# Two more pairs of w2 k tiles in Strassen's form, and two plain pairs whose lo parts arrive by accumulating transfers

## The chip, the cores and the metric

The kernel runs on one core of a Trainium2 chip. The metric is the device time of one execution in microseconds (us), taken from the first to the last instruction; the kernel before was timed in three runs. One more execution was profiled, and every duration below is from that one. PE is the matrix engine, DVE the Vector engine, ACT the Scalar engine, POOL is GpSimd, and SP is the engine that only issues transfers.

## What is computed

Two layers of a decoder trunk over 256 tokens of width 1024, in float32. Each layer is a feed-forward block, a mixer (gated spatial unit beside differential attention) and a second feed-forward block, each followed by a layer norm. The change touches the four feed-forward blocks alone:

```python
def _swiglu(x, w1, w3, w2):
    return (jax.nn.silu(x @ w1) * (x @ w3)) @ w2
...
for l in range(DEPTH):
    h = _swiglu(x, ffn_w1[l, 0], ffn_w3[l, 0], ffn_w2[l, 0])
    x = _layernorm(ALPHA * x + 0.5 * h, ln_g[l, 0], ln_b[l, 0])
    h = _mixer(x, ...)
    x = _layernorm(ALPHA * x + h, ln_g[l, 1], ln_b[l, 1])
    h = _swiglu(x, ffn_w1[l, 1], ffn_w3[l, 1], ffn_w2[l, 1])
    x = _layernorm(ALPHA * x + 0.5 * h, ln_g[l, 2], ln_b[l, 2])
```

The inner width of a feed-forward block is 2816, which is 22 tiles of 128.

## The kernel before

**Three matmuls for one.** A float32 operand is split into a hi part, rounded to a shorter format by ACT (a copy), and a lo part, the remainder, which DVE gets by a subtraction. `three` (L208) then issues hi·hi, lo·hi and hi·lo into one PSUM bank. Weights come from memory as float32 tiles of 128x2048 (1 MB) into one of four `raw` buffers, by a transfer on SP's queue, and are cut there: ACT writes the hi half tile (128x1024), DVE the lo half tile. There are eight hi and eight lo buffers of 128x1024. A `raw` buffer is free for the next transfer when its last cut is done; a hi or lo buffer is free when PE has read it for the last time.

**A feed-forward block** has an up stage and a down stage. The up stage (`gemm_b2`, then `gemm_a2` for nine pairs of inner tiles) makes the 22 inner tiles, and splits each into hi and lo. The down stage multiplies them with w2. A *plain pair* is two inner tiles with 24 matmuls of 128x512: two tiles, two token halves t, two column halves c, three matmuls each (`rows_p`, six matmuls at a time). A *Strassen pair* does the same product with seven blocks in place of eight, so 21 matmuls. Its inner operands are mixed by `mixed` (L559), and its weights by `stream_s` (L280): one raw tile is cut into a (512 columns, L304), b (1024), c (1024) and d (1024), and DVE adds quarters of the raw tile in place between the cuts (L306, L308, L309), so that cut d can be made only after L309, first its hi by ACT and then its lo by DVE. The seven blocks are issued in the order 3, 7, 4, 1, 2, 5, 6 (L631); block 3 and 2 read cut b, 7 and 5 read c, 4 and 6 read d, and 1 reads a. Block 4, the seventh to ninth matmul of the pair, is thus the first to need d, its lo in the eighth matmul. The seven blocks of all Strassen pairs add up in seven banks `S`.

**The down stage's order.** There are `NS = 4` Strassen pairs and seven plain ones. The order on PE is Strassen, plain, Strassen, plain, Strassen, plain, Strassen (L629 to L635). The other four plain pairs are *held*: all of their weights are cut and kept in the hi and lo buffers (eight of each), and PE then goes through (t, c) = (0,0), (0,1), (1,0), (1,1), each with all held pairs (L648 to L655), so that the sums of the first token half are complete when half of the held work is still to come. Beside that, DVE adds the `S` banks to the residual (`more`, L465 and L463; `u`, `v`, L640 and L641) and the four finished banks (`part`, L472), and the layer norm is done for one token half at a time (`finish`, L481).

**From the norm to the next stage.** `finish` starts a task, `turned` (L515), that counts in beats: each `rows_p` or `rows_b` of six matmuls is half a beat, and five of them after (0,1) PE transposes the first half of the normed tokens (L532). ACT scales them into `xf` (L538) and makes the hi part of x, DVE the lo part (L177). The next stage's first matmuls read these. So that the next stage's weights can be cut while the eight buffers still hold the held pairs, its first three half tiles are written to activation slots (`lent = [(0, 1), (0,), (), ()]`, L323; 31 slots of 128x512 in all).

**Order.** PE's order is the program's order, written by hand. A scheduler orders ACT, DVE and POOL ahead of time by priorities; on the chip each engine runs its list strictly in that order, and an instruction that waits holds up all that stand behind it.

## Time and profile before

| | |
|---|---|
| Median of three runs (lowest, highest) | 1230.86 us (1230.62, 1231.16) |
| The profiled execution's own time | 1231.23 us |
| Its span, first to last instruction | 1229.5 us |
| PE busy | 1223.3 us (99%) |
| DVE busy | 980.3 us (80%) |
| ACT busy | 781.1 us (64%) |
| POOL busy | 87.0 us (7%) |
| Granted clock of PE | 1.000 |

The profiled execution is 0.37 us above the median, and 1.7 us of its time lie outside its span. A row of a timeline gives the start, the time to the end of the last of the instructions in it, the engine, the source line, what is written and read, the shape, how many, and in brackets how long the engine was idle before and who ended that. Instructions overlap: the next one starts a little before the end of the one before, so the step from start to start is the rate, and the duration is longer.

### The profile page before, as it was taken

The page shows a single profiled execution, that of the slowest core. Times are in us where ns is not written, and L with a number is a line of the kernel's source. Part 1 is how long each engine was busy: PE and PEld are TensorE (multiplying, and loading weights), DVE is VectorE, ACT ScalarE, POOL GpSimd, SP SyncE. Part 2 cuts the span into 40 slices and gives each one's busy share as a digit, 9 for nine tenths or more (in the row PEclk, how much of TensorE's full clock was granted, in tenths as well). Part 3 has the DMA queues.
Part 4 walks back from the last instruction along what each step waited for, and adds up shares of the span by engine and source line. Part 5 has one row for each costly group of instructions (what it writes and reads, how often), then busy time and mean ns, then how long its engine had stood idle before and what let it go on. Part 6 is the DMA issues. An engine that isn't in the chain of part 4 may idle for free.

```text
span 1229.5 us, 17890 instructions
## 1 busy us (share of the span) xinstructions
PE 1223.3 (99%) x6589; PEld 1050.6 (85%) x6589; DVE 980.3 (80%) x1692; ACT 781.1 (64%) x1424; POOL 87.0 (7%) x184
## 2 busy tenths in 40 slices
PE   9999999999999999999999999999999999999998
PEld 8888888888888888888888888888888888888886
DVE  6877998886587987779978779978866879787886
ACT  6775666679665666656566665566886555766651
POOL 0100000244100000000000000002430000000000
PEclk9999999999999999999999999999999999999999
DMA  9864665654754745546645546656556446455450
GB/s 344 291 205 138 231 217 194 224 167 166 251 178 154 231 159 207 191 138 241 247 178 196 180 142 247 246 188 206 168 174 229 168 171 240 171 206 178 160 211 34
DMA packets 40104, 241.87 MB, mean 197 GB/s; under 512 B 5281, under 2 KB 6353, under 8 KB 13393
## 3 DMA queue, kind: packets, MB, share of 16 engines
q1 hardware_dynamic: 36048, 227.82, 53.2%
q0 software_dynamic: 3536, 12.13, 3.1%
q8 instruction: 51, 0.84, 0.3%
q10 hardware_dynamic: 432, 0.79, 0.2%
q14 instruction: 37, 0.30, 0.1%
HBM read 235.47 MB, written 1.05 MB: 192 GB/s over the span
## 4 chain that ended last, share of the span: by engine, by line
PE 99%; DMA 0%; DVE 0%; ACT 0%; DVEq 0%; issue 0%; ACTq 0%
PE bank L223 38%; PE bank L211 23%; PE bank L230 20%; PE sbank L211 12%; PE bank L371 2%; PE sbank L707 1%; PE sbank L532 1%; PE sbank L756 1%; PE sbank L837 1%; DMA xraw<-in_xT 0%; PE sbank L754 0%; PE sbank L778 0%; PE sbank L585 0%; PE sbank L741 0%; PE sbank L746 0%; PE sbank L504 0%
## 5 line engine op out<-in xcount | busy, mean ns | idle before, releaser
L171 DVE TENSOR_TENSOR wlo<-raw,whi 128x1024 fp32r<-128x1024 f32 (+1 forms) x410 | 450.0, 1116 | 109.1 <-PE bank L230 62.9
L169 ACT ACTIVATE whi<-raw 128x1024 fp32r<-128x1024 f32 (+1 forms) x410 | 388.8, 970 | 186.9 <-PE bank L223 114.8
L223 PE MATMUL bank<-x,whi 128*128 128x512 f32 x1792 | 426.5, 392 | 0.0
L223 PEld LDWEIGHTS bank<-x,whi 128*128 128x128 f32 x1792 | 330.7, 188 | 69.1 <-issue 2.7
L230 PE MATMUL bank<-x,wlo 128*128 128x256 f32 x1792 | 230.0, 284 | 0.0
L230 PEld LDWEIGHTS bank<-x,wlo 128*128 128x128 f32 x1792 | 224.2, 191 | 4.8
L231 ACT ACTIVATE r<-bank 128x256 f32<-128x256 f32 x256 | 96.0, 381 | 67.8 <-PE bank L230 67.4
L211 PE MATMUL bank<-whi,x 128*128 128x512 f32 x328 | 106.6, 394 | 0.0
L293 ACT ACTIVATE shi<-raw 128x1024 fp32r<-128x1024 f32 (+1 forms) x64 | 60.4, 950 | 61.0 <-DVE raw L309 39.1
L295 DVE TENSOR_TENSOR slo<-raw,shi 128x1024 fp32r<-128x1024 f32 (+1 forms) x64 | 69.3, 1088 | 24.8 <-PE bank L230 15.3
L211 PEld LDWEIGHTS bank<-whi,x 128*128 128x128 f32 x328 | 61.6, 188 | 12.7
L211 PE MATMUL sbank<-whi,hhi 128*128 128x512 f32 x168 | 65.7, 391 | 0.0
L211 PE MATMUL sbank<-whi,hlo 128*128 128x512 f32 x168 | 65.4, 389 | 0.0
L211 PE MATMUL sbank<-wlo,hhi 128*128 128x512 f32 x168 | 65.4, 389 | 0.0
L211 PE MATMUL bank<-wlo,x 128*128 128x512 f32 x164 | 64.0, 390 | 0.0
L538 ACT ACTIVATE xf<-sbank,ln_b,ln_g 128x128 f32<-128x128 f32 x80 | 30.1, 456 | 40.8 <-PE sbank L532 40.8
L233 DVE TENSOR_TENSOR silu<-bank,r 128x256 f32<-128x256 f32 x144 | 54.5, 418 | 0.4
L431 POOL DMA_DIRECT2D bc<-in_lng x6 | 3.2, 530 | 728.4 <-DVE bc L430 728.4
L683 POOL TENSOR_TENSOR swap<-swap,sin_t 128x512 f32<-128x512 f32 x16 | 25.0, 1563 | 233.4 <-DMA swap<-z 225.2
L211 PE MATMUL bank<-lhi,x 128*128 128x512 f32 x120 | 39.2, 395 | 0.0
L211 PEld LDWEIGHTS sbank<-whi,hlo 128*128 128x128 f32 x168 | 31.5, 188 | 6.7
L211 PEld LDWEIGHTS sbank<-wlo,hhi 128*128 128x128 f32 x168 | 31.6, 188 | 6.5
(236 smaller groups left out, 1682.3 us busy)
## 6 DMA issues: line engine op xcount, KB each, us to landing
raw<-in_w13a SPq DMA_DIRECT2D x72, 1024.0 KB, 4.9
raw<-in_w2p SPq DMA_DIRECT2D x28, 1024.0 KB, 5.1
raw<-in_wa SPq DMA_DIRECT2D x24, 1024.0 KB, 5.2
raw<-in_w2s SPq DMA_DIRECT2D x16, 1024.0 KB, 4.9
raw<-in_wb SPq DMA_DIRECT2D x16, 1024.0 KB, 5.0
raw<-in_wqk SPq DMA_DIRECT2D x16, 1024.0 KB, 5.2
raw<-in_wbr SPq DMA_DIRECT2D x16, 1024.0 KB, 4.9
raw<-in_w13b SPq DMA_DIRECT2D x12, 1024.0 KB, 5.1
```

The costliest lines, as they stand in the source:

```text
L169: A.activation(h, r, AF.Copy)
L171: V.tensor_tensor(out=w, in0=r, in1=h.bitcast(F32), op=ALU.subtract)
L211: PE.matmul(ps, xx, w, start=start and n == 0, stop=stop and n == 2)
L223: PE.matmul(b[-1], hi[:, k * P : (k + 1) * P], xc(k), start=k == 0, stop=False)
L230: PE.matmul(b[n][:, :T], lo[:, k * P : (k + 1) * P], xc(k)[:, :T], start=False, stop=k == KT - 1)
L231: emptied[0] = A.activation(r[:, s], b[n][:, T:], AF.Copy, scale=scale).ins
L233: a = V.tensor_tensor(out=z[:, s], in0=b[n][:, :T], in1=r[:, s], op=ALU.add)
L293: A.activation(h, r, AF.Copy)
L295: V.tensor_tensor(out=w, in0=r, in1=h.bitcast(F32), op=ALU.subtract)
L371: PE.matmul(ps[t][m], x[:, j, o + t * P : o + (t + 1) * P], y, start=k0 + j == 0 and o == 0 and y is hi, stop=k0 + j == KT - 1 and y is lo)
L538: A.activation(xf[:, s], b[:, s], AF.Identity, scale=self.gT[:, f], bias=self.bT[:, f])
L683: turned_by[0] = G.tensor_tensor(out=s3, in0=s3, in1=s, op=ALU.mult).ins
```

## The change

`NS` becomes 6. The inner tiles 12 to 15 go over from plain to Strassen pairs, so five plain pairs are left, and the order on PE is Strassen, Strassen, plain, Strassen, Strassen, plain, Strassen, Strassen, and then three held pairs. The last Strassen pair's operands lie in the `val` buffers as before, those of the other five in 20 slots.

The first two of the held pairs no longer use the hi and lo buffers. Their weights go to sixteen activation slots, which the finished Strassen pairs have left, in pieces of 128x512. ACT writes each hi piece, and for each lo piece the negated raw value (`scale=-1.0`) in the destination's shorter format; a transfer issued by POOL then reads the same weights from memory a second time and adds them to it in place (`accum_op=ALU.add`), which leaves the remainder. There are eight such transfers of 256 KB in a feed-forward block. DVE has no part in it.

After a feed-forward block `lent` is empty: the next stage's weights all go to the hi and lo buffers. In the up stage a plain pair's two tiles are now collected in `qa` and split at once, 128x512, instead of twice 128x256.

```diff
-NS = 4
+NS = 6
...
-    def stream(src, width=CH, sub=HC, lent=(), after=(None, None)):
+    def stream(src, width=CH, sub=HC, lent=(), after=(None, None), dma=()):
...
                 with behind(latest[0]):
                     A.activation(h, r, AF.Copy)
+                if o // HC in dma:
+                    A.activation(w, r, AF.Copy, scale=-1.0)
+                    G.dma_start(w, src[:, o + p : o + p + sub], accum_op=ALU.add)
+                    continue
                 with behind(after[o // HC] or latest[1]):
                     V.tensor_tensor(out=w, in0=r, in1=h.bitcast(F32), op=ALU.subtract)
...
-            wh, wl = (v[:, j * 512 + c0 : j * 512 + c0 + n] for v in piece)
+            wh, wl = (v[j][:, c0 : c0 + n] if isinstance(v, list) else v[:, j * 512 + c0 : j * 512 + c0 + n] for v in piece)
...
-            lent = [(0, 1), (0,), (), ()]
+            lent = norm.lent
...
+            self.lent = [(0, 1), (0,), (), ()]
...
         for j in range(FB, FT, 2):
+            qa = s512("qa")
             for m, z in gemm_a2([w13a[l, f, j - FB + m] for m in range(2)], both, lambda m: t512("silu")):
                 s = z[:, :T]
                 silu[0] = A.activation(s, s, AF.Silu).ins
-                if (j, j + 1) in SQ:
-                    if m == 0:
-                        qa = s512("qa")
-                    V.tensor_tensor(out=qa[:, m * T : (m + 1) * T], in0=s, in1=z[:, T:], op=ALU.mult)
-                    if m:
-                        mixed((j, j + 1), qa)
-                else:
-                    V.tensor_tensor(out=s, in0=s, in1=z[:, T:], op=ALU.mult)
-                    split(hh(j + m), hl(j + m), s)
+                V.tensor_tensor(out=qa[:, m * T : (m + 1) * T], in0=s, in1=z[:, T:], op=ALU.mult)
+                if m and (j, j + 1) in SQ:
+                    mixed((j, j + 1), qa)
+                elif m:
+                    split(p_hi[j, j + 1], p_lo[j, j + 1], qa)
...
+        ln.lent = [()] * 4
...
-            w = stream(w2p[l, f, PQ.index(q)])
+            slot = hold and len(plain) > 0
+            w = stream(w2p[l, f, PQ.index(q)], sub=512 if slot else HC, lent=(0, 1) if slot else (),
+                       dma=(0, 1) if slot else ())
...
-            if n < NS - 1:
+            if n in (1, 3):
                 plain_pair(False)
```

The diff moves lines, so L306, L308, L309 and L465 of the kernel before are L310, L312, L313 and L470 of the changed one, L295 and L293 are L299 and L297, L171 is L175 and L532 is L537.

Three places in the order of instructions are spoken of below, all in the first feed-forward block; the other three have the same order there. The first is DVE around the last Strassen pair. In the kernel before, the pair's cut d (`slo_1665`) is followed by four cuts of held pairs and then by the first addition of an `S` bank to the residual (`sbank_1425` is the bank of block 7):

```order
L295 TENSOR_TENSOR slo_1663<-raw_1658,shi_1662 128x1024
L308 TENSOR_TENSOR raw_1658<-raw_1658 128x512
L309 TENSOR_TENSOR raw_1658<-raw_1658 128x512
L295 TENSOR_TENSOR slo_1665<-raw_1658,shi_1664 128x1024
L171 TENSOR_TENSOR wlo_1712<-raw_1709,whi_1711 128x1024
L171 TENSOR_TENSOR wlo_1716<-raw_1709,whi_1715 128x1024
L171 TENSOR_TENSOR wlo_1722<-raw_1719,whi_1721 128x1024
L171 TENSOR_TENSOR wlo_1726<-raw_1719,whi_1725 128x1024
L465 SCALAR_TENSOR_TENSOR xtok_144<-xtok_144,sbank_1425 128x512
```

In the changed kernel the same place on DVE reads as follows (`slo_1722` is cut c of the last Strassen pair, `slo_1724` its cut d, `sbank_1436` the bank of block 7):

```order
L299 TENSOR_TENSOR slo_1720<-raw_1717,shi_1719 128x1024
L299 TENSOR_TENSOR slo_1722<-raw_1717,shi_1721 128x1024
L312 TENSOR_TENSOR raw_1717<-raw_1717 128x512
L313 TENSOR_TENSOR raw_1717<-raw_1717 128x512
L470 SCALAR_TENSOR_TENSOR xtok_144<-xtok_144,sbank_1436 128x512
L299 TENSOR_TENSOR slo_1724<-raw_1717,shi_1723 128x1024
L175 TENSOR_TENSOR wlo_1815<-raw_1812,whi_1814 128x1024
```

The addition has moved ahead of cut d of the pair whose block 7 it waits for.

The second place is ACT at the end of the Strassen pairs. In the kernel before, the last pair's cuts b, c and d (`shi_1660`, `shi_1662`, `shi_1664`) stand together, and plain cuts follow:

```order
L293 ACTIVATE shi_1660<-raw_1658 128x1024
L293 ACTIVATE shi_1662<-raw_1658 128x1024
L293 ACTIVATE shi_1664<-raw_1658 128x1024
L169 ACTIVATE whi_1711<-raw_1709 128x1024
L169 ACTIVATE whi_1715<-raw_1709 128x1024
```

In the changed kernel the fifth Strassen pair's cuts c and d (`shi_1681`, `shi_1683`) and then the sixth's b and c (`shi_1719`, `shi_1721`) stand like this on ACT:

```order
L297 ACTIVATE shi_1681<-raw_1675 128x1024
L171 ACTIVATE llo_1772<-raw_1768 128x512
L169 ACTIVATE lhi_1771<-raw_1768 128x512
L171 ACTIVATE llo_1773<-raw_1768 128x512
L169 ACTIVATE lhi_1780<-raw_1768 128x512
L171 ACTIVATE llo_1782<-raw_1768 128x512
L169 ACTIVATE lhi_1781<-raw_1768 128x512
L297 ACTIVATE shi_1683<-raw_1675 128x1024
L297 ACTIVATE shi_1719<-raw_1717 128x1024
L297 ACTIVATE shi_1721<-raw_1717 128x1024
```

Six pieces of the first slot pair (`raw_1768`) now stand between cuts c and d of the fifth pair; six more stand between c and d of the sixth.

The third place is PE between the transposes of the first half of the first token half and the next stage, which is the mixer's. The matmuls that read `x` are the next stage's. In the changed kernel:

```order
L537 MATMUL sbank_1914<-ident,xtok_143 128x128 x4
L215 MATMUL sbank_1442<-whi_1818,hhi_149 128x512
L215 MATMUL sbank_1442<-wlo_1819,hhi_149 128x512
L215 MATMUL sbank_1442<-whi_1818,hlo_154 128x512
L215 MATMUL sbank_1442<-whi_1818,hhi_149 128x512
L215 MATMUL sbank_1442<-wlo_1819,hhi_149 128x512
L215 MATMUL sbank_1442<-whi_1818,hlo_154 128x512
L215 MATMUL bank_1956<-whi_1962,x_1433 128x512
L215 MATMUL bank_1956<-wlo_1963,x_1433 128x512
```

In the kernel before, eighteen matmuls of held pairs and the next four transposes stood there; the end of that stretch is:

```order
L211 MATMUL sbank_1431<-wlo_1746,hhi_151 128x512
L211 MATMUL sbank_1431<-whi_1745,hlo_158 128x512
L532 MATMUL sbank_1883<-ident,xtok_143 128x128 x4
L211 MATMUL bank_1919<-lhi_1925,x_1422 128x512
L211 MATMUL bank_1919<-llo_1927,x_1422 128x512
L211 MATMUL bank_1919<-lhi_1925,x_1422 128x512
```

Between the transposes and the first matmul that reads their result, 18 matmuls and 4 transposes have become 6 matmuls; the next four transposes now come twelve matmuls into the next stage.

More of the change, by code (lines that the diff above doesn't have):

```diff
@@ L553, in ffn @@
         h_hi, h_lo = ({q: act.tile([P, 512], F32R, tag="slot", name=name(n)) for q in PQ} for n in ("hhi", "hlo"))
+        p_hi, p_lo = h_hi, h_lo
         f_hi, f_lo = ([d[k, k + 1] for k in range(0, FB, 2)] for d in (h_hi, h_lo))
@@ L599, in ffn @@
                 silu[0] = A.activation(s, s, AF.Silu).ins
-                if (j, j + 1) in SQ:
-                    if m == 0:
-                        qa = s512("qa")
-                    V.tensor_tensor(out=qa[:, m * T : (m + 1) * T], in0=s, in1=z[:, T:], op=ALU.mult)
-                    if m:
-                        mixed((j, j + 1), qa)
-                else:
-                    V.tensor_tensor(out=s, in0=s, in1=z[:, T:], op=ALU.mult)
-                    split(hh(j + m), hl(j + m), s)
+                V.tensor_tensor(out=qa[:, m * T : (m + 1) * T], in0=s, in1=z[:, T:], op=ALU.mult)
[3 more added lines that the diff above has]
+                    split(p_hi[j, j + 1], p_lo[j, j + 1], qa)
                 if norm is None and j + m == FB:
-                    beside(setup(s[:, :1]), 0)
-        ln = Norm(l, i, 2.0 * ALPHA, 4.0 * EPS, s[:, :1], last)
+                    beside(setup(qa[:, :1]), 0)
+        ln = Norm(l, i, 2.0 * ALPHA, 4.0 * EPS, qa[:, :1], last)
+        ln.lent = [()] * 4
         S = {n: side_bank() for n in (3, 7, 4)}
```

## The prediction

> **What bounds the kernel now.** I read the page's busy shares first, then the chain that ended last.
>
> ```profile
> PE 1223.3 (99%) x6589; PEld 1050.6 (85%) x6589; DVE 980.3 (80%) x1692; ACT 781.1 (64%) x1424; POOL 87.0 (7%) x184
> PE 99%; DMA 0%; DVE 0%; ACT 0%; DVEq 0%; issue 0%; ACTq 0%
> ```
>
> PE is the chain. Its own waits, from the view of waits, are nearly nothing:
>
> ```profile
> PE sbank L383 <- DVE warm L379: 1.0, 1, 1.0
> PE sbank L500 <- DVE xtok L479: 1.0, 1, 1.0
> PE bank L371 <- ACT whi L176: 0.4, 1, 0.4
> PE sbank L504 <- ACT minus L502: 0.2, 1, 0.2
> ```
>
> So a matmul removed is time gained only as long as DVE and ACT still deliver every operand before PE asks for it; any lateness that the change makes is new time. What a matmul is worth stands in the chain in order of time, and how full DVE is in three windows: the up stage with a Strassen pair's mixing, the up stage with a plain pair's split, and one Strassen pair with one plain pair in the down stage (the columns are PE, weight loads, DVE, ACT, POOL, clock, DMA share and GB/s):
>
> ```profile
> 169.38 12.24 PE sbank L211 x54
> 499.99:511.11 11.12, 11.12 (x66) 9.85 (x65) 8.93 (x16) 7.35 (x12) 0.00 (x0) 1.00 0.55 190
> 511.11:522.22 11.11, 11.11 (x65) 9.84 (x65) 7.30 (x13) 7.12 (x12) 0.00 (x0) 1.00 0.57 189
> 140.82:151.02 10.20, 10.20 (x46) 8.45 (x46) 10.13 (x12) 6.55 (x7) 0.00 (x0) 1.00 0.52 181
> ```
>
> 54 matmuls in 12.24 us are 0.2267 us each; the 0.39 us that the groups show for one is its length, of which most overlaps. In the up stage DVE has 2.2 us to spare in 11.1, so two more mixed pairs there cost nothing: I put them at zero, and without that cover each would cost 1.6 us (8.93 less 7.30). In the down stage DVE is as busy as PE. That is the place.
>
> **The gain.** Each Strassen pair has 3 matmuls fewer, two more pairs in four feed-forward blocks make 24, and 24 x 0.2267 is 5.4 us. A measurement of this kernel tells 0.2%, 2.5 us, from no change.
>
> **DVE in the down stage.** These rows are DVE's timeline in the first block, and PE's first Strassen matmul there:
>
> ```profile
> 128.39 0.40 PE L211 MATMUL sbank<-shi,shh 128*128 128x512 f32 x1
> 135.70 1.23 DVE L295 TENSOR_TENSOR slo<-raw,shi 128x1024 fp32r<-128x1024 f32 x1 [1.19 <-ACT shi L293]
> 136.85 2.35 DVE L171 TENSOR_TENSOR wlo<-raw,whi 128x1024 fp32r<-128x1024 f32 x2
> ...
> 144.58 0.68 DVE L295 TENSOR_TENSOR slo<-raw,shi 128x512 fp32r<-128x512 f32 x1
> 145.30 1.22 DVE L306 TENSOR_TENSOR raw<-raw 128x1024 f32<-128x1024 f32 x1
> 146.44 1.22 DVE L295 TENSOR_TENSOR slo<-raw,shi 128x1024 fp32r<-128x1024 f32 x1
> 147.58 2.35 DVE L171 TENSOR_TENSOR wlo<-raw,whi 128x1024 fp32r<-128x1024 f32 x2
> 149.85 2.35 DVE L295 TENSOR_TENSOR slo<-raw,shi 128x1024 fp32r<-128x1024 f32 x2
> 152.12 0.68 DVE L308 TENSOR_TENSOR raw<-raw 128x512 f32<-128x512 f32 x1
> 152.84 0.69 DVE L309 TENSOR_TENSOR raw<-raw 128x512 f32<-128x512 f32 x1
> 154.74 1.23 DVE L295 TENSOR_TENSOR slo<-raw,shi 128x1024 fp32r<-128x1024 f32 x1 [1.21 <-ACT shi L293]
> 155.88 3.49 DVE L171 TENSOR_TENSOR wlo<-raw,whi 128x1024 fp32r<-128x1024 f32 x3
> ```
>
> From start to start a 1024-column step is 1.14 us (146.44 to 147.58), a 512-column one about 0.6, and 0.72 where the next needs its result (144.58 to 145.30, 152.12 to 152.84). A Strassen pair is four 1024 steps, of which one is the sum L306, and cut a and two sums at 512: 4.56 and 1.8, together 6.4 us. A plain pair is 2.3 us. PE needs 21 x 0.2267, 4.76 us, and 5.44 us. In the old order DVE has 8.7 us of work for 10.2 us of PE; in the new one, two Strassen pairs and a plain one, 15.1 us for 14.96. On top comes the hop from L309 through ACT and back before cut d, in which DVE stood idle for 1.2 us at 154.74; in a double pair one of two such hops can be filled with the other pair's sum L306, the other stays. So DVE loses about 1.3 us in each period, and lives on what it is ahead.
>
> How far ahead it is: at 136.85 DVE had done the first two Strassen pairs, the first plain pair and all that was left of the up stage. In the new order this is the same work, in another sequence and with the hop of 1.19 us partly filled, so I take 135.9. The third and fourth pair then take 12.7 us, one hop of 1.3 and the small dependences 0.4: the fourth's cut d is done at 150.4. PE reaches the fourth pair at 128.39 + 87 x 0.2267 = 148.1 and wants d's lo seven matmuls later, at 149.7: **0.8 us** of waiting, between 0 and 1.6 with the start of DVE's count. The second plain pair ends on DVE at 152.6, and the fifth pair's steps up to L309 take 7.0 us with the sixth's early steps that the scheduler puts between them: 159.6.
>
> Here ACT comes in, with these rows, and the time from issue to landing of a weight tile (KB, us):
>
> ```profile
> 153.65 1.06 ACT L293 ACTIVATE shi<-raw 128x1024 fp32r<-128x1024 f32 x1 [3.52 <-DVE raw L309]
> 166.23 3.22 ACT L169 ACTIVATE lhi<-raw 128x512 fp32r<-128x512 f32 x6
> ```
>
> ```profile
> raw<-in_w2p SPq DMA_DIRECT2D x28, 1024.0 KB, 5.1
> ```
>
> A 1024 copy takes ACT 1.06 us and a 512 piece 3.22 / 6 = 0.54. Cut c of the fifth pair is made from 156.0 on: it waits for its sum, a step of 1.22 us from 154.3, and stands behind a piece of the slot pair, whose raw buffer is free with the fourth pair's cut d at 150.4 and filled at 155.5. Behind cut c stand six slot pieces, 3.2 us, and then cut d. So d's hi runs from 160.2 to 161.25 and d's lo to 162.5, where PE, now 0.8 us late, wants it at 128.39 + 139 x 0.2267 + 0.8 = 160.7: **1.9 us**, between 1 and 2.5.
>
> The sixth pair has a wait that doesn't depend on how far ahead DVE is. In its order the addition of bank 7 (L470) stands ahead of cut d's lo, so d can't be made until PE has finished block 7, and PE wants d right behind block 7. Two rows show how soon DVE starts behind a matmul that ends a bank:
>
> ```profile
> 185.80 0.39 PE L211 MATMUL sbank<-whi,hlo 128*128 128x512 f32 x1
> 186.23 0.69 DVE L472 TENSOR_TENSOR xtok<-xtok,sbank 128x512 f32<-128x512 f32 x1 [0.28 <-PE sbank L211]
> ```
>
> 0.43 us after that matmul's start, then a step of 0.60, then 1.23 for d: 2.26 us, where PE's second matmul behind it would start after 0.45. That is **1.8 us** in every block, and no less. Behind L470 on DVE stand this cut, the last held pair's cuts and the next stage's; all slide with it. The three waits are 4.5 us a block, 18.0 in four.
>
> **The accumulating transfers.** They take two held pairs off DVE, 4.6 us a block, which I count nowhere on the path: that work lay behind the last Strassen pair. Their own price is not in the trace. This row comes nearest, a plain transfer of the same size on POOL's queue:
>
> ```profile
> wsT<-in_sguwT POOLq DMA_DIRECT2D x4, 256.0 KB, 6.0
> ```
>
> The last pieces are written by ACT some 1.1 us behind the sixth pair's cut d, at about 168.5, and wanted at 128.39 + 199 x 0.2267 + 4.5 = 178.0, so 9.5 us are there. I take 6.0 as it stands and the price as nothing; twice that would be 2.5 us late, and more with a queue before it. They can't speed PE up, so no gain is in it. The Trainium skill, in DMA: Bandwidth & Descriptors (Anatomy of one DMA, the gpsimd path), has a GpSimd transfer cost about 2.0 us and its bytes at 436 GB/s, an estimate of 2.6 us for 256 KB. By that even four transfers in a row would be in time, and the sum the same; the row is more than twice the page's figure and decides, so lateness keeps a chance below.
>
> **From the norm to the next stage.** Three of the four blocks have a stage behind them. Before, in the first block, from PE's transposes to x:
>
> ```profile
> 181.46 0.60 PE L532 MATMUL sbank<-ident,xtok 128*128 128x128 f32 x4
> ...
> 186.04 0.60 PE L532 MATMUL sbank<-ident,xtok 128*128 128x128 f32 x4
> 186.39 0.48 PE L211 MATMUL bank<-lhi,x 128*128 128x512 f32 x1
> ```
>
> ```profile
> 182.20 1.49 ACT L538 ACTIVATE xf<-sbank,ln_b,ln_g 128x128 f32<-128x128 f32 x4
> 183.57 0.64 ACT L169 ACTIVATE whi<-raw 128x512 fp32r<-128x512 f32 x1
> 184.09 0.64 ACT L176 ACTIVATE x<-xf 128x512 fp32r<-128x512 f32 x1
> ```
>
> ```profile
> 185.27 0.69 DVE L177 TENSOR_TENSOR x<-xf,x 128x512 fp32r<-128x512 f32 x1
> ```
>
> x's hi part was ready 3.27 us after the transposes began and its lo part 4.5 us after (4.0, had DVE been free); the first reader came after 4.93 us, so all was covered. Now transposes (0.35 us, 186.04 to 186.39) and 6 matmuls, 1.71 us, lie between. PE waits 1.6 us for the hi part, and two matmuls later 0.3 to 0.7 for the lo part: **2.1 us**, between 1.8 and 2.4, or 6.3 in three. The norm itself keeps its 30 matmuls of cover up to the transposes; it was done 0.9 us ahead of them,
>
> ```profile
> 179.55 1.00 DVE L488 TENSOR_SCALAR xtok<-xtok,mv,nwy 128x512 f32<-128x512 f32 x2
> ```
>
> and since PE is held up as much as DVE I take it at nothing, up to 2 us each if DVE's backlog lasts. The empty `lent` takes no buffers from the next stage that it needs: two held pairs have left theirs. The joined split in the up stage saves about 0.1 us of DVE's time per plain pair, nothing on the path.
>
> **Sum.** 18.0 + 6.3 - 5.4 is 18.9 us over the profiled execution's own 1231.23, so 1250.1; that execution lay 0.37 above the median, which gives 1249.7, and I say 1250.
>
> **Rivals.** *Only the waits that the order forces.* DVE keeps ahead and the first two waits of each block vanish: 4 x 1.8 + 6.3 - 5.4 is 8 us, 1239. For it speaks that my count of DVE's lead is good to 1 us; against it, 15.1 us of work for 14.96. *The transfers land late.* If an accumulating transfer takes twice the row's 6.0 us, the last pieces are 2.5 us late, and 4 us with the wait of one for the other, in each block: 16 us more, 1266. Nothing in the profile speaks for or against. By the Trainium skill, TensorE: Matmul & The Clock Gate (Part 1), PE drops to half clock after an idle window of about 3.4 us; none of my waits is that long, no run here shows it, and only this case would grow by it. *Faster: PE's queue hides the waits.* The 24 matmuls are gone in any case; if the seven waits together were under 2.9 us the kernel would gain over 0.2%, and with none it runs in 1225. The place that decides is cut d of the last pair: L470 would have to find block 7 ended about 1.8 us before PE wants block 4, which PE's order excludes; only a misread order makes this true. *A draw.* Waits between 3 and 8 us in all: 1231. That the matmuls don't go is no case: the order of instructions shows 24 fewer.
>
> **Chances.** Forecast 0.64, forced waits alone 0.13, late transfers 0.11, faster 0.06, draw 0.06. The forecast's own bounds (0 to 1.6, 1 to 2.5, 1.8 to 2.2, 1.8 to 2.4, and the norm's 0 to 2) run from 1242 to 1263; the range reaches to the forced waits below and the late transfers above, 1237 to 1266. Slower by over 0.2% are the first three, 0.88.
>
> **What would show it.** In the changed profile PE's waits should list DVE `slo` (L299) in fours: a wait of 1.8 us in the last pair's block 4 each time, with L470 just before on DVE; about 2 us in the fifth pair, behind ACT's `lhi` and `llo` pieces; under 1 in the fourth. Next to these, waits of 1.6 us for ACT's x and under 1 for DVE's x, three times. PE's waits should come to about 24 us. I am wrong if PE waits for a transfer `llo`, if the fourth and fifth pairs show no wait, or if PE's idle time is under 5 us.

## The result and the profile after

The changed kernel takes 1279.46 us (median of 5 runs, 1276.77 to 1281.49) against 1230.93 for the one before: ratio 1.039, 95% interval 1.038 to 1.041. It is slower, as forecast, but by 48.5 us and not by 19, and lies outside the range. The profiled execution took 1276.77, the quickest of the five, with a span of 1274.7; the working below goes by spans, 45.2 us over the 1229.5 of before.

The page of the changed kernel, busy share of PE and the chain that ended last:

```profile
PE 1235.6 (97%) x6565; PEld 1049.0 (82%) x6565; DVE 1009.1 (79%) x1728; ACT 811.7 (64%) x1476; POOL 114.6 (9%) x216
PE 62%; issue 20%; DMA 6%; DVE 6%; ACT 4%; POOL 1%; DVEq 0%; ACTq 0%; POOLq 0%
```

PE is no longer the whole chain: transfers, DVE and ACT have parts of it. The 20% of issue are no lost time: 86.5 us from 977 on and 139.2 us from 1068 on make the most of them, and PE was busy without a gap in both stretches. PE is also busy 12 us longer with 24 matmuls fewer, so some of them ran slower. PE's waits say on what (us in total, times, longest):

```profile
PE bank L215 <- DMA llo<-in_w2p: 16.3, 6, 3.2
PE sbank L215 <- DVE slo L299: 11.8, 13, 1.5
PE bank L215 <- ACT x L180: 3.7, 3, 1.2
...
PE sbank L215 <- ACT shi L297: 0.5, 2, 0.3
```

The largest is what the prediction named as its refutation: PE waits for a transfer `llo`, six times, twice in each of the first three blocks. These are the rows of PE's timeline in the first block, from its first Strassen matmul to the first reader of x:

```profile
128.63 0.40 PE L215 MATMUL sbank<-shi,shh 128*128 128x512 f32 x1
...
150.57 0.50 PE L215 MATMUL sbank<-slo,shh 128*128 128x512 f32 x1 [0.44 <-DVE slo L299]
...
162.38 0.50 PE L215 MATMUL sbank<-slo,shh 128*128 128x512 f32 x1 [0.76 <-DVE slo L299]
...
169.12 0.50 PE L215 MATMUL sbank<-slo,sv 128*128 128x512 f32 x1 [1.48 <-DVE slo L299]
...
172.24 0.39 PE L215 MATMUL bank<-shi,sv 128*128 128x512 f32 x1
...
177.31 0.65 PE L215 MATMUL bank<-llo,hhi 128*128 128x512 f32 x1 [3.09 <-DMA llo<-in_w2p]
...
181.12 0.80 PE L215 MATMUL bank<-llo,hhi 128*128 128x512 f32 x1 [2.31 <-DMA llo<-in_w2p]
...
182.14 0.63 PE L215 MATMUL bank<-whi,hhi 128*128 128x512 f32 x1
182.56 0.63 PE L215 MATMUL bank<-wlo,hhi 128*128 128x512 f32 x1
...
197.05 0.40 PE L215 MATMUL sbank<-whi,hlo 128*128 128x512 f32 x1
198.69 0.50 PE L215 MATMUL bank<-whi,x 128*128 128x512 f32 x1 [1.24 <-ACT x L180]
```

Two things are read from the starts. After the two waits for `llo` the steps are 0.42 to 0.43 us (182.14 to 182.56) and not 0.2267: half the clock. And the down stage can be cut in two and each part set against 0.2267 us for every matmul in it: the Strassen part, from 128.63 to the last Strassen matmul at 172.24, takes 43.61 us where 173 steps are 39.22, so 4.4 are lost; the held part, from there to 197.05, takes 24.81 where 72 steps are 16.32 and 0.49 goes, as in the kernel before, to two slower restarts around transposes, so 8.0 are lost. The same in all four blocks:

| us lost | block 1 | 2 | 3 | 4 | sum |
|---|---|---|---|---|---|
| Strassen part | 4.4 | 4.3 | 4.2 | 6.3 | 19.2 |
| held part | 8.0 | 7.6 | 8.4 | 0.0 | 24.0 |
| from there to the next down stage, over before | 2.3 | 1.9 | 3.1 | – | 7.3 |

The sum is 50.5; less 5.4 for the 24 matmuls, and with 0.2 ahead of the first down stage, it is 45.3, the difference of the spans to 0.1 us. So nothing is missing, and the question is the held part.

The transfers themselves, in the window of the first block's tail (155 to 200 us) and then of the last block's (1230 to 1275):

```profile
raw<-in_wb SPq DMA_DIRECT2D x4, 1024.0 KB, 10.4
...
llo<-in_w2p POOLq DMA_DIRECT2D x8, 256.0 KB, 11.0
```

```profile
llo<-in_w2p POOLq DMA_DIRECT2D x8, 256.0 KB, 7.5
```

They land 11.0 us after issue at the median of the first block, where the prediction took 6.0, and 7.5 in the last, where no next stage follows and PE doesn't wait for them. Which transfers they meet shows in the queue of SP and the issues of POOL, first block:

```profile
163.51 10.57 SPq L156 DMA_DIRECT2D raw<-in_wb  x4
```

```profile
164.82 0.87 POOL L172 DMA_DIRECT2D llo<-in_w2p  x1 [0.16 <-issue]
165.86 0.87 POOL L172 DMA_DIRECT2D llo<-in_w2p  x1 [0.17 <-PE bank L215]
```

The next stage's 4 MB are issued from 163.51 on, in the middle of the accumulating transfers. The two pieces of the second slot pair that were issued at 164.82 and 165.86 let PE go on at 177.31 and 181.12; without waiting, PE would have read them at 174.1 and 174.7, 9.2 and 8.9 us after their issue. They took 12.4 and 15.2 us:

```profile
llo<-in_w2p POOLq DMA_DIRECT2D x1, 256.0 KB, 12.4
llo<-in_w2p POOLq DMA_DIRECT2D x1, 256.0 KB, 15.2
```

Issued 1.04 us apart, they landed 3.8 us apart, so the second came in behind the first. In the 4 us around the second wait's end, the DMA share (next to last column; the clock stands ahead of it) is full and the clock is half:

```profile
180.00:184.00 4.00, 2.88 (x7) 2.30 (x8) 0.00 (x0) 2.19 (x4) 0.00 (x0) 0.50 1.04 334
```

### The profile page after: what moved, and what is told of

Read it like the earlier page. It is cut to its first block, busy times and chain, and to the rows that moved or that the text cites. A ratio compares the mean times of both kernels' runs of the same rounds, so it can differ in the third digit from the quotient of the medians.

```text
span 1274.7 us, 18074 instructions
## 1 busy us (share of the span) xinstructions
PE 1235.6 (97%) x6565; PEld 1049.0 (82%) x6565; DVE 1009.1 (79%) x1728; ACT 811.7 (64%) x1476; POOL 114.6 (9%) x216
## 4 chain that ended last, share of the span: by engine, by line
PE 62%; issue 20%; DMA 6%; DVE 6%; ACT 4%; POOL 1%; DVEq 0%; ACTq 0%; POOLq 0%
PE bank L227 27%; PE bank L234 13%; PE bank L215 13%; PE sbank L215 4%; DMA llo<-in_w2p 4%; DVE slo L299 3%; PE bank L375 2%; ACT shi L297 2%; DMA raw<-in_w2p 1%; PE sbank L713 1%; DMA bc<-in_lng 1%; PE sbank L537 1%; DVE raw L313 1%; ACT lhi L169 1%; ACT llo L171 0%
## 5 line engine op out<-in xcount | busy, mean ns | idle before, releaser
L175 DVE TENSOR_TENSOR wlo<-raw,whi 128x1024 fp32r<-128x1024 f32 (+1 forms) x396 | 425.6, 1092 | 96.3 <-PE bank L234 45.7
L169 ACT ACTIVATE whi<-raw 128x1024 fp32r<-128x1024 f32 (+1 forms) x396 | 366.5, 946 | 196.7 <-PE bank L227 113.8
L215 PE MATMUL bank<-whi,x 128*128 128x512 f32 x400 | 129.9, 396 | 3.7 <-ACT x L180 3.7
L299 DVE TENSOR_TENSOR slo<-raw,shi 128x1024 fp32r<-128x1024 f32 (+1 forms) x96 | 102.2, 1089 | 22.1 <-ACT shi L297 11.3
L297 ACT ACTIVATE shi<-raw 128x1024 fp32r<-128x1024 f32 (+1 forms) x96 | 87.2, 944 | 48.4 <-DVE raw L313 22.9
L215 PEld LDWEIGHTS bank<-wlo,x 128*128 128x128 f32 x200 | 37.6, 188 | 7.2
L606 ACT ACTIVATE silu<-silu 128x256 f32<-128x256 f32 x72 | 29.5, 410 | 15.7 <-DVE silu L237 15.7
L172 POOL DMA_DIRECT2D llo<-in_w2p x32 | 27.8, 878 | 122.5 <-ACT llo L171 119.0
L723 ACT ACTIVATE pp<-pp,mx 128x256 f32<-128x256 f32 (+1 forms) x64 | 28.3, 444 | 14.6 <-DVE mx L721 14.6
L169 ACT ACTIVATE lhi<-raw 128x512 fp32r<-128x512 f32 x44 | 26.2, 618 | 8.7 <-DMA raw<-in_w2p 8.7
```

The lines of the kernel that those rows point to most:

```text
L169: A.activation(h, r, AF.Copy)
L175: V.tensor_tensor(out=w, in0=r, in1=h.bitcast(F32), op=ALU.subtract)
L215: PE.matmul(ps, xx, w, start=start and n == 0, stop=stop and n == 2)
L297: A.activation(h, r, AF.Copy)
L299: V.tensor_tensor(out=w, in0=r, in1=h.bitcast(F32), op=ALU.subtract)
L606: silu[0] = A.activation(s, s, AF.Silu).ins
```

## The experiments

Theories: **contention** (the transfers are late since they share the DMA engines with the next stage's tiles), **accumulation** (an accumulating transfer is slow however free the engines are), **clock** (the half clock behind the waits costs about 2 us a block of its own), and **VectorE** (its chain of sums and cuts sets the waits in the Strassen part). The runs' losses are worked out as in the table above; `...` in a diff marks lines left out.

**next_held.** The next stage's tiles wait for bank 6 (GpSimd copies one column into each tile, so that the transfer must follow it):

```diff
+            G.tensor_copy(raw[:, :1], late)      # late = u[:, :1]
         nc.sync.dma_start(raw[:, :width], src)
```

> The change with one thing added: the four weight tiles of the next stage (4 MB) start only when GpSimd has copied one column of u into them, after bank 6 is read, so that the accumulating transfers of the slot pairs have the DMA engines without them. Contention theory: the transfers land in 7.5 us or less, as they do in the last block, where no next stage follows (10.2 to 11.1 us in blocks 1 to 3); TensorE's six waits for llo (16.3 us) and the half clock after them go, about 7.7 us in each of three blocks, 23 in all: 1256 us, range 1252 to 1262. Rival (the accumulation itself is slow, however free the engines are): the six waits stay at 2 us and over, 1275 to 1280 us. Second rival: the held tiles are now late themselves, and TensorE waits for whi at the next stage's start, over 1265 us with the llo waits gone.

Measured 1258.62 us, ratio 1.0225 (1.021 to 1.024). PE's waits, the first two rows:

```profile
PE sbank L217 <- DVE slo L301: 11.7, 13, 1.5
PE sbank L540 <- DVE xtok L496: 5.2, 3, 2.4
```

No wait for `llo` is left, and the transfers land in 6.8 us (median). Something new takes 5.2 us: the transposes wait for the norm, because DVE, which serves its queue in order, now meets the late tiles' cuts. The held part still loses 5.9 us by it, so some 1253 us would be left without it, within the forecast's range. In the first block the half clock follows here too (0.50 from 192 to 198 us, behind a wait of 1.86 us), and the way from the norm to the next down stage is 1.9 us longer than in the changed kernel. Contention is confirmed; that accumulating is slow enough by itself is refuted for this kernel.

**plain_transfer.** The same bytes from the same place, without the accumulation (lo then holds the whole weight; the remainder is left out of the result):

```diff
-                    G.dma_start(w, src[...], accum_op=ALU.add)
+                    G.dma_start(w, src[...])
```

> The change with the slot pairs' transfers as plain copies of the same bytes from the same place, without accumulation (lo then holds the whole weight instead of its rest, so this part of the result changes; the amount of work does not). Rival (accumulation itself is slow): the waits for llo go, 1256 us. Contention theory: the plain copies still share the engines with 4 MB of the next stage, but they take less of them: the accumulating ones moved 8.39 MB in about 757 engine-us (6.7% of 16 x 1274.7 less 3.1% of 16 x 1229.5), 11 GB/s for one engine, where the other transfers of the same queue made 20; at that rate a block's 2.1 MB take 6.6 us of all 16 engines and not 11.8. So the waits shrink by half or more but need not go: 1256 to 1270 us, likeliest 1262. If they stay as they are, 1277 us, only the bytes and the place in the queue count.

Measured 1258.35 us, ratio 1.024 (1.021 to 1.026). Landing, the queue's packets, MB and share of the 16 engines' time, and PE's wait:

```profile
llo<-in_w2p POOLq DMA_DIRECT2D x32, 256.0 KB, 4.8
```

```profile
q0 software_dynamic: 8144, 20.52, 5.3%
```

```profile
PE sbank L215 <- DMA llo<-in_w2p: 3.4, 2, 1.8
```

The queue's share with accumulation, and in the kernel before:

```profile
q0 software_dynamic: 8144, 20.52, 6.7%
```

```profile
q0 software_dynamic: 3536, 12.13, 3.1%
```

The waits fall from 16.3 to 3.4 us; they don't vanish, but nearly. So either cure, free engines or plain copies, takes most of the loss away in this kernel. The same two pieces (the fifth and sixth transfer of a block), which PE asked for 9.2 and 8.9 us after issue, show why. Their times from issue to landing:

| us | next stage's tiles beside them (block 1) | no such tiles |
|---|---|---|
| accumulating | 12.4 and 15.2 (changed kernel) | 7.6 and 7.8 (next_held, block 1); 7.9 and 8.1 (changed kernel, last block) |
| plain | 9.1 and 8.6 (plain_transfer) | 3.8 and 4.1 (plain_transfer, last block) |

Either burden alone just fits into about 9 us; the two together don't.

**lo_on_dve.** VectorE makes these lo parts, no transfers:

```diff
-                       dma=(0, 1) if slot else ())
+                       dma=())
```

> The change without the accumulating transfers: VectorE makes the slot pairs' lo by eight subtractions of 128x512 (0.6 us apart) in each block, and ScalarE's eight negated pieces (0.52 us apart) go. Both theories of the transfers: no wait for a DMA llo, full clock, minus 23 us. VectorE theory: its queue in the stage grows by 4.9 us, of which some lies ahead of the last Strassen cut; the Strassen waits for slo grow by 1 to 2 us a block, and x comes up to 2 us later: 1256 + 4 x 1.5 + 3 x 1 = 1265, range 1254 to 1272. If ScalarE's relief weighs more (the fifth pair's cut d stood behind its slot pieces), 1252 us or less.

Measured 1257.32 us, ratio 1.021 (1.020 to 1.023). The held part loses 0.1 us in each of blocks 1 to 3 and nothing in the last, the Strassen part 6.0, 4.5, 6.0 and 8.5. The transfers had bought VectorE 5.9 us in four blocks and cost 24.0.

**transfers_alone.** The other part of the change by itself: four Strassen pairs, three plain ones among them, four held, the first two of these in slots:

```diff
-NS = 6
+NS = 4
...
-            slot = hold and len(plain) > 0
+            slot = hold and len(plain) > 1
...
-            if n in (1, 3):
+            if n < NS - 1:
```

> Four Strassen pairs as before the change, but two of the four held pairs in slots, with lo from accumulating transfers, and no slots lent to the next stage. Contention theory: no wait in the Strassen part (VectorE has its plain pairs between), the waits for llo in blocks 1 to 3 as in the change, 4 to 8 us a block with the half clock, none in block 4, x not later since four pairs are held: 1231 + 3 x 6 = 1249, range 1240 to 1256. Accumulation-itself rival: the same waits in block 4 as well, 1231 + 4 x 6 = 1255. No-cost rival (the prediction's price, nothing): 1231.

Measured 1271.89 us, ratio 1.034 (1.032 to 1.035). A clear miss of the forecast, on the costly side, and in the last block too (6.7 us):

```profile
PE bank L215 <- DMA llo<-in_w2p: 29.4, 7, 6.8
```

**alone_plain** and **alone_next_held** take away one cause each, by the two edits shown above, from transfers_alone.

> Four Strassen pairs and two of the four held pairs in slots, as in the run of the transfers alone (1271.9 us; its held part longer than before the change by 11.6, 12.5, 12.8 and, in the last block, 6.7 us), with plain copies of the same bytes in place of the accumulating transfers (lo then holds the whole weight: a part of the result changes, no work does). If the accumulation's double use of the engines is what makes them late: 2 us or less in the last block and 2 to 4 in the others, 1231 + 10 = 1241 us, range 1233 to 1246. If it is the place in the queue and the bytes: over 1260 us. If plain copies are never waited for: 1231 us.

> The run of the transfers alone, accumulating, with the next stage's four weight tiles held back until bank 6 is read. If these tiles are the whole of the difference between blocks 1 to 3 (11.6 to 12.8 us) and the last block (6.7): 6.7 us in each, 1231 + 4 x 6.7 = 1258 us, range 1252 to 1262, unless the held tiles are late themselves. If only the accumulation counts: 1272 us as without it. If only the next stage's tiles counted, 1231 + 6.7 = 1238.

Measured 1253.18 us, ratio 1.016 (1.013 to 1.019), and 1236.39 us, ratio 1.0043 (1.0028 to 1.0058). PE's waits, first of alone_plain, then of alone_next_held:

```profile
PE bank L215 <- DMA llo<-in_w2p: 14.4, 6, 4.1
```

```profile
PE bank L217 <- DMA llo<-in_w2p: 2.4, 4, 1.5
```

| us lost in the held part | block 1 | 2 | 3 | 4 |
|---|---|---|---|---|
| transfers_alone | 11.6 | 12.5 | 12.8 | 6.7 |
| alone_plain | 5.7 | 8.5 | 9.4 | 0.0 |
| alone_next_held | 0.6 | 0.0 | 0.9 | 4.0 |

Both forecasts missed, and the table shows what each cause does. In blocks 1 to 3 there is no loss to speak of without the next stage's tiles: 0.9 us or less is left, with the accumulation in place. With them plain copies are late too in this kernel (5.7 to 9.4 us), and the accumulation makes what is lost there 1.4 to 2 times as much. The profiled execution of alone_plain is the longest of its four (1246.81 to 1255.36 us), so its row lies at the upper end. In the last block, with no next stage, plain copies lose nothing, so the accumulation is needed for the loss; but it doesn't act by the landing time alone. In transfers_alone the last three of the stage's own weight tiles (`raw<-in_w2p`) land in 8.4 to 11.8 us there, beside the first slot pair's transfers, and in 5.4 to 7.7 with plain copies; and the second pair's transfers go out only 3.9 us ahead of the last Strassen matmul (4.4 in alone_next_held), where it is 6.9 with plain copies and 8.7 in the first block. How large the loss is there is uncertain: 6.7 and 4.0 us in two profiles of a block in which the kernels don't differ.

**clock_kept.** Matmuls of zeros fill PE's waits for the second slot pair, so that it doesn't stand idle:

```diff
+            for _ in range(fill[j]):             # 52 and 40, in blocks 1 to 3
+                PE.matmul(ps[:, :P], warm, warm, start=False, stop=False)
```

> The change with 92 small matmuls of zeros (128x128, bf16, added to bank 2, which they leave as it is) in blocks 1 to 3 at the place where TensorE waits for the second slot pair's llo: 52 ahead of its first half, 40 ahead of its second. Estimate 0.06 us each (a quarter of the columns of a 0.2267 us step): 3.0 and 2.3 us, about the two waits (2.2 to 3.2 us each). Clock theory: the slow steps of 0.427 us that follow the waits come from TensorE's having been idle; they cost about 0.2 us on 9 to 10 matmuls a block, 6 us in three blocks, and go: 1273 us, granted clock 1.00, the transfers as late as before. Rival: the clock falls for another reason (load, the DMA's traffic) and stays at 0.50 there, 1279 us. If a small matmul takes 0.11 us as at the program's start, the filling is longer than the waits and adds 3 to 5 us a block: 1285 us or more.

Measured 1279.16 us, ratio 1.039 (1.037 to 1.041): no gain. The window of the first block that showed half the clock:

```profile
180.00:184.00 4.00, 3.49 (x21) 2.71 (x19) 3.26 (x6) 2.19 (x4) 0.00 (x0) 1.00 1.06 326
```

The mechanism is right: with PE kept at work the clock is now 1.00. Its price isn't: PE got ahead and found the next piece missing, at a place where the changed kernel had not waited.

```profile
187.30 0.50 PE L215 MATMUL sbank<-llo,hhi 128*128 128x512 f32 x1 [1.51 <-DMA llo<-in_w2p]
```

SP's queue in this run, and then in the changed kernel, shows a part of why:

```profile
181.50 0.33 SPq L156 DMA_DIRECT2D raw<-in_wqk  x1
```

```profile
187.89 0.33 SPq L156 DMA_DIRECT2D raw<-in_wqk  x1
```

A tile buffer came free 6.4 us sooner, and the next weight tile joined the transfers that were still under way. That this is what delayed the last piece is argued from the order of times, not shown by a run of its own.

**fewer_adds.** No transfers (lo stays the negated weight), and two of the three sums of each Strassen pair left out:

```diff
-                    G.dma_start(w, src[...], accum_op=ALU.add)
...
-        V.tensor_tensor(out=raw[:, 1024:1536], in0=raw[:, :512], in1=raw[:, 1024:1536], op=ALU.add)
-        V.tensor_tensor(out=raw[:, 1536:], in0=raw[:, 1024:1536], in1=raw[:, 1536:], op=ALU.add)
```

> The change without the accumulating transfers (the slot pairs' lo stays the negated weight) and without two of the three additions that make the last cut of a Strassen pair (raw[1024:1536] and raw[1536:]); these two parts of the result are left out, the work of TensorE and ScalarE stays. Without the transfers alone the time would be about 1255 us (plain copies 1258, lo by VectorE 1257). VectorE theory: its chain of additions and cuts, 6.5 us for a pair against TensorE's 4.76, sets the waits in the Strassen part (4.2 to 4.4 us in blocks 1 to 3, 6.2 in block 4, 19 in all); 1.2 to 1.4 us less for each pair takes the most of them: the Strassen part 39.5 to 41 us instead of 43.6, 1255 - 14 = 1241 us, range 1237 to 1246. Rival (ScalarE's hi cuts, behind its slot pieces, or the tiles' arrival set the waits): the part stays over 42.5 us, 1250 us or more.

Measured 1233.02 us, ratio 1.0015 (1.0006 to 1.0024), better than its range. PE's waits:

```profile
PE bank L214 <- ACT x L179: 3.7, 3, 1.2
PE sbank L384 <- DVE warm L380: 1.0, 1, 1.0
```

No wait for `slo` or `shi` is left; the Strassen part takes 39.28 us for 39.22 of matmuls. So without these two sums, and the hops that they force, nothing of the 19 us is left. This run also closes the account: with 5.4 us gained and, in this profile, 7.0 lost on x and behind it, 1.6 should be left; the spans differ by 1.1 us and the medians by 2.1, so it closes to 0.5.

**bank7_behind.** No transfers (lo stays the negated weight), and the addition of bank 7 behind the last cut d:

```diff
+        with behind(lastcut[0]):
-        ln.more(1, 0, S[7], ALU.subtract, ln.scale)
+            ln.more(1, 0, S[7], ALU.subtract, ln.scale)
```

> The change without the accumulating transfers (the slot pairs' lo stays the negated weight, a part of the result left out), and with the addition of bank 7 to the residual set behind the last cut d on VectorE. The prediction held that this addition, ahead of the cut, makes the sixth pair wait 1.8 us. If it alone does: 1.96 us a block go, 1255 - 8 = 1247 us. Chain theory (the cut stands behind ScalarE's hi cut, and that behind the last of the three additions): only the addition's own 0.6 to 0.7 us go, 2.6 us in four blocks: 1252.5 us. If the cut waits for something later still, nothing: 1255 us.

Measured 1253.61 us (1250.75 in the profiled execution), ratio 1.018 (1.016 to 1.019). The Strassen part loses 3.5, 3.6, 3.5 and 6.6 us: 17.1 in all where plain_transfer, alike but for this edit and its copies, loses 19.6. That is 0.9 to 1.0 us less in each of blocks 1 to 3 and 0.3 more in the last, 2.5 in all, near the 2.6 of the chain theory; the longest wait for `slo` is halved and not gone:

```profile
PE sbank L215 <- DVE slo L299: 8.9, 13, 0.8
```

The prediction had the addition as the sole cause of the sixth pair's wait. It is one of two things in a row: cut d was late anyway. A part of the saving is lost again further on: PE now waits 1.2 us for DVE's lo part of x, and from the held part to the next down stage the three blocks lose 8.3 us and not 7.4.

**ns5, ns5_pool, ns5_pool2, ns6_held4.** Attempts at a better version, with four held pairs in ordinary buffers, so that x isn't late, and no transfers: five Strassen pairs; the same with one and with two of the sums on GpSimd; six pairs with one plain pair among them.

```diff
-NS = 6
+NS = 5                                          # ns6_held4: 6, and "if n == 3" for the plain pair
...
-        V.tensor_tensor(out=raw[:, 1024:1536], ...)
+        G.tensor_tensor(out=raw[:, 1024:1536], ...)   # ns5_pool; the next sum too in ns5_pool2, ns6_held4
...
-        ln.lent = [()] * 4
...
-            w = stream(w2p[l, f, PQ.index(q)], sub=512 if slot else HC, ...)
+            w = stream(w2p[l, f, PQ.index(q)])
```

> Five Strassen pairs, in the order S S P S S P S, then four held plain pairs in the ordinary buffers as before the change; no slots in the down stage, no transfers, the next stage's slots lent as before. Gain 3 matmuls x 4 blocks x 0.2267 = 2.7 us. The tail is that of the kernel before, so x is not later. VectorE theory: the two places with two Strassen pairs side by side cost 0.7 us at the fourth pair, as in the change, and up to 1 at the fifth: 1231 - 2.7 + 4 x 1.2 = 1233 us, range 1229 to 1237. Rival: any step beyond four pairs costs as much as in the change (19 us of waits for two pairs, so some 9 for one), 1238 us.

> Five Strassen pairs and four held pairs as in the run before it, with one of the three additions of each Strassen pair (raw[1024:1536]) on GpSimd, which is idle in the stage and took 1.56 us for 128x512 in the rotary step. VectorE's queue is 3 us shorter by the held part. VectorE theory: the wait of the held pairs for wlo (5.7 us a block with the slow steps behind it) shrinks by about 3 us: 1231 - 2.7 + 4 x 2.5 = 1238 us, range 1233 to 1244. Rival (GpSimd's addition takes longer than VectorE's and stands in the chain to cut d; or VectorE is slowed while GpSimd works): the waits move into the Strassen part, 1245 us or more.

> The same with two of the three additions (raw[1024:1536] and raw[1536:]) on GpSimd. VectorE's queue is 6 us shorter, no wait for wlo or slo is left but the first ones: 1231 - 2.7 = 1228.5 us, range 1227 to 1233, which would be faster than both kernels. Rival: two additions of 1.56 us in a row (3.1 us and the hand-over twice) make the last cut of a pair late, 0.5 to 2 us at the second of two neighbours: 1233 to 1240.

> Six Strassen pairs with only one plain pair among them (S S S S P S S), four held pairs in ordinary buffers, two additions on GpSimd, no transfers. x is not later, since four pairs are held. TensorE needs 34.0 us for the part, VectorE about 5.3 us for a Strassen pair and 2.5 for a plain one, 34.3, and then the held cuts. If that is all: 1231 - 5.4 + 4 x 1 = 1229.5 us. VectorE theory: no slack is left and the four held pairs' cuts and the additions to the residual (16 us of VectorE) come behind it, so the held part waits 2 to 4 us a block: 1237 us, range 1229 to 1244.

Measured 1256.99 (ratio 1.020, 1.018 to 1.022), 1248.73 (1.0142, 1.013 to 1.016), 1257.06 (1.021, 1.020 to 1.023) and 1300.16 (1.056, 1.055 to 1.058): all slower than the kernel before, all above their forecasts. The first row of PE's waits in ns5, in ns5_pool and in ns6_held4:

```profile
PE bank L215 <- DVE wlo L175: 14.5, 4, 3.6
```

```profile
PE bank L215 <- DVE wlo L175: 6.0, 5, 3.6
```

```profile
PE bank L215 <- DVE wlo L175: 17.2, 8, 4.6
```

x is in time again (the first reader starts 0.59 us behind the last held matmul, as before the change, and not 1.64), but DVE's backlog, small in the Strassen part (0.8 us in blocks 1 to 3, 3.4 in the last), comes out at the held pairs' cuts: 5.7 us a block, 6.7 in the last. Moving one sum to GpSimd takes most of that away in three blocks (1.2 us are left there, 7.3 in the last), and the Strassen part loses 1.0 us more in each. Moving the second spoils it again: the Strassen part now loses 4.8 to 6.3 us a block. Two things stand against it. VectorE's cuts are slower beside the sums (those of 1024 columns and of 512 in ns5, then in ns5_pool2, with the second sum on GpSimd):

```profile
L299 DVE TENSOR_TENSOR slo<-raw,shi 128x1024 fp32r<-128x1024 f32 x60 | 72.4, 1223 | 8.2 <-ACT shi L297 6.1 <-PE bank L234 1.5
...
L299 DVE TENSOR_TENSOR slo<-raw,shi 128x512 fp32r<-128x512 f32 x20 | 13.8, 689 | 9.1 <-PE bank L234 9.1
```

```profile
L299 DVE TENSOR_TENSOR slo<-raw,shi 128x1024 fp32r<-128x1024 f32 x60 | 80.7, 1357 | 31.9 <-ACT shi L297 31.8
...
L299 DVE TENSOR_TENSOR slo<-raw,shi 128x512 fp32r<-128x512 f32 x20 | 18.9, 947 | 10.9 <-PE bank L234 9.1 <-ACT shi L297 1.8
```

```profile
L313 POOL TENSOR_TENSOR raw<-raw 128x512 f32<-128x512 f32 x20 | 36.6, 1828 | 1.6
```

And the two sums stand one behind the other ahead of cut d, at 1.5 and 1.8 us on GpSimd where VectorE took 0.69 for each: ACT then waits on GpSimd's sums and DVE on ACT (31.8 us, where it was 6.1). How much of the loss each of the two makes was not separated. ns6_held4 loses 11.8 to 12.1 us a block in the Strassen part and 6.1 to 8.2 in the held part. No version found here beats the kernel before.

## Where the prediction was right and where it failed

- **The gain** of 5.4 us: right, as the account shows that closes with it.
- **DVE in the down stage**, 4.5 us a block, 18.0: right in sum, 4.2 to 4.4 in blocks 1 to 3 and 6.3 in the last, 19.2; nor is the order wrong (0.7 for the fourth pair, 1.6 for the fifth, 2.0 for the sixth in the first block, forecast 0.8, 1.9 and 1.8). The view of waits gives less, 11.8 + 0.5 us, since it counts from the modelled end of the matmul before: the wait of 1.48 us sets two starts 1.85 us further apart than 0.2267, and the next step is another 0.11 longer. What was wrong is the reason given for the sixth: "no less" than 1.8 for the addition ahead of cut d; alone it made 1.0 a block at most, so that the sixth pair's size came out is in part luck. That the last block loses 2 us more was not foreseen, and which of its differences does it wasn't tried.
- **From the norm to the next stage**, 2.1 us at each of three boundaries: measured 1.8 at the first (1.41 where PE waits for x, 0.4 in the steps behind), and 1.9 to 3.1 up to the next down stage, 7.3 for the 6.3 forecast. A part of that lies in the mixer, where PE now waits 0.7 us once for `hb`.
- **The accumulating transfers**: this is the step that failed. "I take 6.0 as it stands and the price as nothing" was 24.0 us. The 9.5 us that it found between issue and use were nearly there (9.2 and 8.9 for the two pieces that PE waited for); the duration wasn't: 11.0 us at the median of the first block, and 12.4 and 15.2 for those two. The row of 6.0 us was of plain copies, two at a time, and the engines were busy there too; this is the window from the issue to the landing of its first copy in the kernel before (DMA share 0.83):

```profile
307.67:313.60 5.93, 5.93 (x37) 5.22 (x37) 3.03 (x5) 4.65 (x10) 2.25 (x5) 1.00 0.83 270
```

So a look at the share of busy engines would not have told the two places apart. What differs is that the transfers accumulate, that eight of them come in a row, and that four tiles of the next stage run beside them; by the table under plain_transfer the first and the last of these are each worth 3.3 to 7.4 us for a piece. The prediction took the plain row for want of another, and did not ask what else would be in flight. It said itself that lateness would come "with a queue before it"; the tiles were in sight, as the kernel before loads them in the same stretch. The Trainium skill says in DMA: Bandwidth & Descriptors (Issuing engines are not separate DMA queues) that transfers started by different engines run on the same 16 DMA engines and interleave. The trace agrees: the tiles' own landing went from 5.0 to 7.8 us in the median (`raw<-in_wb`).
- **The rival of late transfers** named the mechanism's place, but priced it at 4 us a block in four blocks. It is 8 us in three and nothing in the last, where no tiles of a next stage are in flight.
- **The clock**, in the same rival: PE did fall to half clock behind these waits. But with the clock kept up the kernel was no faster (clock_kept, 1279.16 and 1279.46 us): PE then waited for later pieces. That the transfers set the time of the stretch, and not PE, fits this, but the earlier tile of the next stage in that run leaves it unproven.
- **Sums.** Three slips of the working change nothing: by its own times the fifth pair's wait is 162.5 less 160.7, 1.8 us and not 1.9; four transfers in a row at 2.6 us each are 10.4, more than the 9.5 that it had; and its upper bounds add up to 1264 us and not 1263.

What stays open: why exactly each piece lands when it does (the order in which the engines serve the two queues is not in the trace), and the size of the accumulation's own loss in a block without a next stage.

## What to carry to other kernels

The landing time of a transfer holds for its kind and for the load of its place: before a transfer is priced by a row from elsewhere, look up what stands ahead of it in its own queue, what the other queues have in flight between its issue and its use, and whether the row is of the same kind. A slow stretch that ends in a wait for something else may cost nothing; removing it here only led to later waits. And where two engines are equally full, a saving on the one can be given back at the next place where the other's backlog meets a deadline.

## What the runs showed of the hardware

- An accumulating transfer took about 1.6 times the DMA engines' time of a plain one of the same bytes (1.8 times in transfers_alone against alone_plain: 6.5% of 16 x 1273.3 us and 5.0% of 16 x 1253.3, each less the 610 us of before). With accumulation the queue's share rose from 3.1% of 16 x 1229.5 us to 6.7% of 16 x 1274.7, 757 us of one engine for 8.39 MB; with plain copies from 3.0% of 16 x 1256.2 (lo_on_dve) to 5.3% of 16 x 1255.9, 462 us. That is 11 and 18 GB/s for one engine.
- The half clock came 0.2, 1.2 and 0.7 us after the end of the first wait for `llo` in blocks 1 to 3, that is after waits of 3.09, 2.19 and 3.17 us, and held for 6.8 us each time (177.5 to 184.3, 617.8 to 624.7 and 812.4 to 819.2); the second wait fell into this time. In next_held it came 1.5 us after a wait of 1.86 us. The Trainium skill, in TensorE: Matmul & The Clock Gate (Part 1), speaks of an idle window of about 3.4 us that runs freely; shorter idle times were enough here.
- VectorE's own steps were slower with GpSimd's sums of 128x512 in the stage: with two sums on GpSimd a cut of 1024 columns took 1357 ns on average and not 1223, one of 512 took 947 and not 689, and GpSimd's second sum took 1.83 us.
